# No identity matmuls in PE's waits, B's sum on GpSimd, output blocks and gelu in the first stage's own buffers

## The chip, the cores and the metric

One core of a Trainium2 chip runs the whole program. The metric is device time in microseconds (us), from one launch of the kernel. PE is TensorE, DVE VectorE, ACT ScalarE, POOL GpSimd, and SP the engine that only issues DMAs.

## What is computed

A hidden state of 256 tokens by 1024 columns goes through eight stages in fp32: an S5 state-space mixer with a gated output, a feed-forward block, a stick-breaking attention, a second feed-forward block, and then twice a hybrid layer with its feed-forward block. The change lies in the first stage, up to the gelu:

```python
dt = jnp.exp(log_dt)[:, None]
mag = jnp.exp(lam_re * dt)                       # 64 groups, 64 states each
lbar_re, lbar_im = mag * jnp.cos(lam_im * dt), mag * jnp.sin(lam_im * dt)
...
bb_re, bb_im = _cmul(coef_re[..., None], coef_im[..., None], b_re, b_im)
bu_re = jnp.einsum('blgh,gph->lbgp', u, bb_re)   # and bu_im
_, _, s_re, s_im = lax.associative_scan(_ssm_combine, (a_seq_re, a_seq_im, bu_re, bu_im), axis=0)
y = jnp.einsum('lbgp,ghp->blgh', s_re, c_re) - jnp.einsum('lbgp,ghp->blgh', s_im, c_im)
y = y.reshape(bsz, seq, D_MODEL) + d_skip * x
h = jax.nn.gelu(y)
val, gate = jnp.split(h @ w_glu, 2, axis=-1)
z = val * jax.nn.sigmoid(gate)
```

## The kernel before, in words

`s5_states` computes everything up to the gelu, and leaves the result transposed and split into a high and a low half (`xTh`, `xTl`). `main_stream` then runs all the large matmuls, three for each product (high by high, low by high, high by low). Its weights come in tiles of 512 KB: a DMA into one of the four buffers of the pool `raws`, a copy to the high half on ACT (`wh`), two subtractions for the low half on DVE (`wl`).

In `s5_states` the sequence is cut into 32 chunks of 8 tokens. The parts, with the names that the order uses:

- The start, in the order of the code: DMAs of the parameters, of B, C and x; powers 1 to 8 of lambda on DVE (`LR`), their sum and difference `PRs`, `PRd` in the PSUM tile `lt[0]`, and on ACT the negated real part `nPRr` in the PSUM tile `lt[1]` and copies `LRs`, `LRd` in SBUF. PE transposes B and C; ACT copies B to `Br`, `Bi`; PE sums both once more into `both`, which ACT copies to `Bs` (the real plus the imaginary part).
- `ug`, `ut`, `us`: x is regrouped (ACT), transposed (PE) and stored as `u` (ACT).
- For each of eight blocks of groups: three products `vp` on DVE (B times powers of lambda), their transposes `vt` on PE (four of 128x128 each), stores `vs` on ACT into `vT`; then `sm`, `sd`, `st`, `ss` (PE, ACT, PE, ACT) give the chunk states; `ss7` is the last.
- `cp`, `cs`: C times the coefficient, on DVE. `wp`: 24 products of C and powers of lambda on POOL, into the tiles `W` and `wd`; `dm` the skip blocks on POOL.
- `lp`, `lc`, `lw`: the response within a chunk (PE), copied into `kz` (ACT), and spread by 16 small DMAs for each half into the tile `lag`.
- `mg`, `bo`: the scan over the chunks, on DVE alone; its multipliers lie in `lt[1]` (`bp`, `bt` make them).
- For each half f: `tm` and three `om` on PE give the outputs, `os` copies them (the output blocks `yc`), `ot` transposes on PE, `og` is the gelu on ACT, `oh` and `ol` the two halves of the result. `sx` makes the difference of the states that the third `om` reads.
- `wd`, `wh`, `wl`: a first weight tile for `main_stream`, loaded and split within the stage.

The order of all these steps on each engine is written out in the table `ORDER`. An entry `=12` of it issues 12 matmuls of the identity with 64 columns of itself, into columns 448 to 511 of `lt[1]`, which nothing reads (line 728); there are 159 of them. A PSUM tile that PE writes is not read by DVE at the same time, whatever its columns. The four buffers of `raws` hold in turn `Bs` with the skip blocks, the first weight tile, the output blocks and the gelu of either half, and then the weights of `main_stream`.

The lines which the rows name: 249 transposes of B and C, 322 B's sum on PE, 341 and 357 lambda's powers on DVE, 409 `ug`, 415 `ut`, 461 `vp` and `wp`, 477 `Bd` (the difference of B's parts), 495 `vt`, 499 `vs`, 512 and 527 `sd` and `ss`, 563 to 566 `mg` and `bo`, 651 `tm`, 664 `om`, 685 `oh`, 717 `wl`, 728 the identity matmuls, 779 the weights' high half in `main_stream`, 822 to 824 its three matmuls.

Of the kernel before, what the change touches and what calls it, by code (L numbers as in the profile page):

```python
# [12 lines left out]
F32 = mybir.dt.float32  # L13
# [6 lines left out]
P = 128  # L20
# [146 lines left out]
cp00 cp01 =12 dt ug0 =29 ut0 cp10 vp01 ds cp11 vt01 bm ug1 us00 us01 vp02 wd vs01 ut1 us10 =1 vt02 vp00 dk vp12 vs02  # L167
vp10 cs2 vp11 vt00 ut2 vs00 bp0 vt12 vp22 dm vp20 us11 vs12 vt10 sm0 vt11 vp21 vs10 us20 wp12 vt22 sd0 vs11 vp30 ut3
vs22 st0 vp31 us30 ss0 vt21 vt20 vs21 vs20 cs1 bt0 cs0 lz1 wr0 wp02 sm1 vt31 vp40 lz0 wp22 vs31 wp32 vp32 wp31 vt30
vs30 wp01 sd1 vp42 wp20 lz2 wp21 vp41 sm2 sd2 vt40 vt32 vs40 wp11 st1 vs32 vp50 st2 wp30 wp00 vt42 ss1 lz3 wp10 vp52  # L170
vt41 vp60 bp1 ss2 sm3 vs42 vt52 vs41 vp61 wr1 wp62 vt50 sd3 vp51 vs52 sm4 wp40 bt1 vs50 vt60 wp71 st3 sd4 vs60 ss3 bp2
st4 ss4 us31 us21 wh0 vt61 vt51 wh1 vs51 vs61 vp70 lp0 lc110 vp62 lc010 wp70 lc000 vp72 vp71 wp61 lc101 lc100 vt62
vt71 lc011 wp60 vs62 lc111 wl1 =18 sm5 vt70 vs71 sd5 bp3 =4 vt72 lw1 wp41 wp42 wp72 lc001 vs70 wp51 vs72 =2 st5 ss5
sm6 mg00 sm7 sd6 wl0 st6 sd7 lw0 mg01 =4 st7 ss6 wp50 ss7 wp52 =5 lp1 mg02 lc310 mg10 lc300 mg11 lc301 lc311 lc200 lw3
lc201 mg12 lc211 bo0 bo1 bo2 bo3 lc210 =40 tm0 bo04 bo05 =12 om00 =1 om01 bo14 lw2 sx0 =1 om02 hd bo15 os01 os00 =12
ot01 ot00 sx1 og00 og01 oh01 =7 tm1 =1 om10 =1 om11 =1 om12 oh00 os10 os11 =8 ot11 og11 ot10 ol01 ol00 og10 oh10 oh11
ol10 ol11
# [3 lines left out]
def s5_states(nc, tc, a, V, S, G, T, const, raws, ats, hpool, mm_ps, tp_ps, xts, ident, load_h, **_):  # L181
# [11 lines left out]
    def buf(tag, shape):  # L193
        return z.tile(shape, F32, name=tag, tag=tag, bufs=BUFS[tag])
# [15 lines left out]
    with tc.manual_schedule(engines=PAP):  # L210
# [108 lines left out]
        both = tp_ps([P, SH, NGP])  # L319
        for hh in range(SH):  # L320
            for i, raw in enumerate(b_raw):
                T.matmul(both[:, hh, :], raw[:, :, hh], i32, start=(i == 0), stop=(i == 1))
        S.copy(Bs, both.rearrange("p h g -> p g h"))
# [43 lines left out]
        def step(name, fn, *args):  # L367
            steps[name] = lambda: fn(*args)

        def first(key, make):  # L370

            if key not in tl:
                tl[key] = make()
            return tl[key]
# [21 lines left out]
        def gelu(f):  # L396
            return first(("gel", f), lambda: raws.tile([P, 4, NC, TC], F32, name="raw", tag="raw"))
# [78 lines left out]

        step("bm", lambda: G.tensor_sub(Bd, Br, Bi))
# [19 lines left out]
        def v_store(i, k):  # L497
            vT = first(("vT", i), lambda: buf("vT", [P, 3, 4, P]))
            (V.tensor_copy if (i, k) in DVE_V else S.copy)(vT[:, k], tl["pv", i, k])
# [167 lines left out]
        def state_out_store(f, b):  # L667
            yc = first(("yc", f), lambda: raws.tile([P, TC, 8, SH], F32, name="raw", tag="raw"))
            (V.tensor_copy if f * b else S.copy)(yc.rearrange("p j (g e) h -> p g j e h", e=2)[:, :, :, b, :],
                                       tl["pc", f][b].rearrange("p g (j h) -> p g j h", h=SH))  # L670
# [53 lines left out]
        with tc.manual_schedule(engines={mybir.EngineType.DVE}):  # L724
            for name in ORDER.split():
                if name[0] == "=":
                    for _ in range(int(name[1:])):
                        T.matmul(lt[1][:, 448:], ident, ident[:, :64], start=True, stop=True)  # L728
                else:
                    steps.pop(name)()  # L730
# [816 lines left out]
```

## Time and profile before

| | us |
|---|---|
| median of 3 runs (1412.14 to 1417.54) | 1415.89 |
| the profiled execution | 1417.67 |
| its span in the trace | 1415.9 |
| PE busy in the span | 1382.7 (98%) |
| DVE, ACT, POOL busy | 905.5, 688.2, 80.3 |
| identity matmuls (line 728) busy on PE | 51.6 |

The first stage lasts until about 142 us of the span. A row of the timeline gives the start and the length of a group of like instructions, and behind it, in brackets, how long the engine stood idle before it and whose end it waited for. Matmuls overlap, so the length of one is not the step from one to the next: a row's length divided by its count is nearer to the step. Each fp32 matmul or transpose with an identity that is not a transposing one shows as two records, so the 12 matmuls of `=12` are 24 records. [...]

### The profile page before, as it was taken

Reading aid. Unit: us, or ns where it says so; the run is one execution under the profiler, and the core shown is the slowest. Engines: PE = TensorE matmul, PEld = TensorE weight load, DVE = VectorE, ACT = ScalarE, POOL = GpSimd, SP = SyncE. Lnnn points to the kernel's source line nnn. Section 1 sums busy time; section 2 is a strip of 40 time slices with the busy share of each in tenths; the row PEclk is TensorE's granted clock in tenths of the full one; section 3 lists DMA queues with packets and bytes.
Section 4 is the critical chain, followed back from the end, with each engine's and each line's share of the span. In section 5 each row is a group of like instructions: output and inputs, shape, how many; then the busy total and the mean of one; then the engine's idle time right before and its main releaser. Section 6 shows DMA issues by size and latency. Waiting matters only on the chain.

```text
span 1415.9 us, 21753 instructions
## 1 busy us (share of the span) xinstructions
PE 1382.7 (98%) x8009; PEld 1155.0 (82%) x8009; DVE 905.5 (64%) x1881; ACT 688.2 (49%) x1065; POOL 80.3 (6%) x149
## 2 busy tenths in 40 slices
PE   7988999999999999999999999999999999999998
PEld 7987878888888878888787888888888888888887
DVE  5472767555588686555699658655568866856463
ACT  1531654444468745444446545544545654545451
POOL 1420000000001110000020000000001000000000
PEclk9997999999999999999999999999999999999999
DMA  5163957555564436665455555646555554655551
GB/s 135 61 69 103 292 168 232 185 179 178 194 193 156 140 119 214 193 197 191 120 162 160 181 177 184 200 152 208 177 157 174 148 161 153 202 186 174 182 195 58
DMA packets 143403, 237.38 MB, mean 168 GB/s; under 512 B 15744, under 2 KB 84800, under 8 KB 142656
## 3 DMA queue, kind: packets, MB, share of 16 engines
q1 hardware_dynamic: 143296, 235.99, 53.8%
q8 instruction: 63, 1.03, 0.3%
q14 instruction: 44, 0.36, 0.1%
HBM read 228.35 MB, written 1.05 MB: 162 GB/s over the span
## 4 chain that ended last, share of the span: by engine, by line
PE 91%; DVE 5%; DMA 1%; ACT 1%; issue 1%; POOL 0%; SPq 0%; ACTq 0%; DVEq 0%; POOLq 0%
PE acc L824 8%; PE acc L823 8%; PE acc L822 8%; PE mm_ffn_g_t L823 5%; PE mm_ffn_g_t L824 5%; PE mm_ffn_g_t L822 5%; PE mm_ff_g_t L822 4%; PE mm_ff_g_t L824 4%; PE mm_ff_g_t L823 4%; PE lt L728 3%; PE tp L881 2%; PE mm_hy_t L823 2%; PE mm_hy_t L822 2%; PE mm_hy_t L824 2%; PE mm_s_g_t L822 1%; PE mm_hy_b_t L824 1%
## 5 line engine op out<-in xcount | busy, mean ns | idle before, releaser
L785 DVE TENSOR_TENSOR wl<-raw,wh 128x512 fp32r<-128x512 f32 (+1 forms) x834 | 541.8, 685 | 150.1 <-ACT wh L779 133.3
L779 ACT CAST wh<-raw 128x1024 fp32r<-128x1024 f32 (+1 forms) x417 | 436.4, 1048 | 246.7 <-DMA raw<-in_ffn_w_gu_dram 42.4
L822 PE MATMUL acc<-wh,bTh 128*128 128x512 f32 x544 | 213.2, 392 | 0.0
L823 PE MATMUL acc<-wh,bTl 128*128 128x512 f32 x544 | 211.9, 390 | 0.3
L824 PE MATMUL acc<-wl,bTh 128*128 128x512 f32 x544 | 212.1, 390 | 0.0
L822 PE MATMUL mm_ffn_g_t<-wh,xTh 128*128 128x512 f32 x352 | 140.5, 399 | 1.9 <-ACT xTh L867 1.9
L823 PE MATMUL mm_ffn_g_t<-wh,xTl 128*128 128x512 f32 x352 | 137.5, 391 | 0.4 <-DVE xTl L868 0.4
L824 PE MATMUL mm_ffn_g_t<-wl,xTh 128*128 128x512 f32 x352 | 137.4, 390 | 0.0
L868 DVE TENSOR_TENSOR bTl<-tp,bTh 128x256 fp32r<-128x256 f32 (+1 forms) x104 | 52.6, 512 | 124.4 <-ACT bTh L867 124.4
L823 PEld LDWEIGHTS acc<-wh,bTl 128*128 128x128 f32 x544 | 102.2, 188 | 21.7 <-DVE bTl L868 1.0
L824 PEld LDWEIGHTS acc<-wl,bTh 128*128 128x128 f32 x544 | 102.1, 188 | 21.3
L822 PEld LDWEIGHTS acc<-wh,bTh 128*128 128x128 f32 x544 | 102.2, 188 | 21.0 <-ACT bTh L867 0.3
L867 ACT CAST bTh<-tp 128x256 fp32r<-128x256 f32 (+1 forms) x104 | 45.3, 444 | 149.0 <-PE tp L881 135.6
L822 PE MATMUL mm_ff_g_t<-wh,xTh 128*128 128x512 f32 x256 | 102.6, 401 | 0.0
L824 PE MATMUL mm_ff_g_t<-wl,xTh 128*128 128x512 f32 x256 | 99.9, 390 | 0.0
L823 PE MATMUL mm_ff_g_t<-wh,xTl 128*128 128x512 f32 x256 | 99.7, 389 | 0.0
L822 PEld LDWEIGHTS mm_ffn_g_t<-wh,xTh 128*128 128x128 f32 x352 | 66.1, 188 | 14.9 <-ACT xTh L867 2.4
L823 PEld LDWEIGHTS mm_ffn_g_t<-wh,xTl 128*128 128x128 f32 x352 | 66.2, 188 | 13.8 <-DVE xTl L868 1.1
L824 PEld LDWEIGHTS mm_ffn_g_t<-wl,xTh 128*128 128x128 f32 x352 | 66.1, 188 | 13.8
L822 PE MATMUL mm_hy_t<-wh,xTh 128*128 128x512 f32 (+1 forms) x160 | 61.4, 384 | 0.8 <-DVE at L1328 0.6
L823 PE MATMUL mm_hy_t<-wh,xTl 128*128 128x512 f32 (+1 forms) x160 | 59.8, 374 | 1.5 <-DVE xTl L868 1.3
L824 PE MATMUL mm_hy_t<-wl,xTh 128*128 128x512 f32 (+1 forms) x160 | 59.8, 374 | 0.0
(475 smaller groups left out, 2136.0 us busy)
## 6 DMA issues: line engine op xcount, KB each, us to landing
raw<-in_w_ff_dram SPq DMA_DIRECT2D x128, 512.0 KB, 4.5
raw<-in_ffn_w_gu_dram SPq DMA_DIRECT2D x176, 256.0 KB, 4.1
raw<-in_w_in_dram SPq DMA_DIRECT2D x64, 512.0 KB, 4.4
raw<-in_ffn_w_down_dram SPq DMA_DIRECT2D x44, 512.0 KB, 4.9
raw<-in_ssm_w_glu_dram SPq DMA_DIRECT2D x32, 256.0 KB, 3.9
raw<-in_sb_w_qkv_dram SPq DMA_DIRECT2D x32, 256.0 KB, 3.8
raw<-in_w_out_dram SPq DMA_DIRECT2D x16, 512.0 KB, 4.3
raw<-in_ssm_w_out_dram SPq DMA_DIRECT2D x8, 512.0 KB, 4.5
```

Of the source, the lines that this page charges most:

```text
L728: T.matmul(lt[1][:, 448:], ident, ident[:, :64], start=True, stop=True)
L779: S.copy(wh, raw)
L785: V.tensor_sub(l2[:, sl], r2[:, sl], h2[:, sl])
L822: T.matmul(ps, xh[:, k], wh, start=first, stop=False)
L823: T.matmul(ps, xl[:, k], wh, start=False, stop=False)
L824: T.matmul(ps, xh[:, k], wl, start=False, stop=last)
L867: S.copy(hi, ps)
L868: V.tensor_sub(lo, ps, hi)
L881: T.transpose(pt[:, k, :], src[:, k * P:(k + 1) * P], ident)
```

## The change

All identity matmuls go, with the branch that issues them. B's sum goes from PE (32 matmuls in `both`, and a copy on ACT) to POOL, as one addition of `Br` and `Bi`. The output blocks `yc` take a buffer of `vT`, and the gelu one of `u`, so that both leave the pool `raws`. The table `ORDER` is written anew; two lines of it are shown.

```diff
 ORDER = """
-cp00 cp01 =12 dt ug0 =29 ut0 cp10 vp01 ds cp11 vt01 bm ug1 us00 us01 vp02 wd vs01 ut1 us10 =1 vt02 vp00 dk vp12 vs02
...
+ug1 vp12 ut2 vp11 cp10 cp00 bm vt12 bs ug0 us20 cp11 ut3 us21 cp01 vt11 vp10 vs12 cs2 vt10 wp12 us31 vp02 vp01 cs1
...
-        both = tp_ps([P, SH, NGP])
-        for hh in range(SH):
-            for i, raw in enumerate(b_raw):
-                T.matmul(both[:, hh, :], raw[:, :, hh], i32, start=(i == 0), stop=(i == 1))
-        S.copy(Bs, both.rearrange("p h g -> p g h"))
...
-            return first(("gel", f), lambda: raws.tile([P, 4, NC, TC], F32, name="raw", tag="raw"))
+            return first(("gel", f), lambda: buf("u", [P, 4, NC, TC]))
...
+        step("bs", lambda: G.tensor_add(Bs, Br[:, :NGP], Bi[:, :NGP]))
         step("bm", lambda: G.tensor_sub(Bd, Br, Bi))
...
-            vT = first(("vT", i), lambda: buf("vT", [P, 3, 4, P]))
+            vT = first(("vT", i), lambda: buf("vT", [P, 3 * 4 * P]).rearrange("p (k q n) -> p k q n", k=3, q=4))
...
-            yc = first(("yc", f), lambda: raws.tile([P, TC, 8, SH], F32, name="raw", tag="raw"))
+            yc = first(("yc", f), lambda: buf("vT", [P, 3 * 4 * P])[:, :TC * P].rearrange("p (j g h) -> p j g h", j=TC, g=8))
...
-                if name[0] == "=":
-                    for _ in range(int(name[1:])):
-                        T.matmul(lt[1][:, 448:], ident, ident[:, :64], start=True, stop=True)
-                else:
-                    steps.pop(name)()
+                steps.pop(name)()
```

PE's instructions from the transposes of C to the first transposes of a product `v`, before (lines 249 and 322 belong to the start, 434 is `dt`):

```order
L249 MATMUL pv<-ident,c_136 128x32 x16
L322 MATMUL tp<-ident,big_134 128x32 x32
L728 MATMUL lt_124<-ident 128x64 x12
L434 MATMUL tp<-ident,dpad 64x32 x2
L728 MATMUL lt_124<-ident 128x64 x29
L415 MATMUL tp<-ident,xTh 128x128 x4
L495 MATMUL pv<-ident,v 128x128 x4
```

The same place on PE now (the line numbers are those of the changed code: 248 was 249, 409 was 415, 490 was 495):

```order
L248 MATMUL pv<-ident,c_136 128x32 x16
L409 MATMUL tp<-ident,xTl 128x128 x4
L490 MATMUL pv<-ident,v 128x128 x4
L409 MATMUL tp<-ident,xTl 128x128 x4
L490 MATMUL pv<-ident,v 128x128 x8
```

The sum of B and the first 41 identity matmuls are gone from ahead of the first transposes, and the second half of x comes first.

PE's instructions from the end of `lp1` to the second half's `om`, before (624 ends `lp1`, 651 is `tm`, 664 `om`, 676 `ot`, 822 the first matmul of the gated unit):

```order
L624 MATMUL mm<-raw,pick 32x4x16 x8
L728 MATMUL lt_124<-ident 128x64 x40
L651 MATMUL mm<-lag_585,u 32x128 x32
L728 MATMUL lt_124<-ident 128x64 x12
L664 MATMUL mm<-big_587,c_1238 32x128 x32
...
L728 MATMUL lt_124<-ident 128x64 x12
L676 MATMUL tp<-ident,raw 128x128 x8
L728 MATMUL lt_124<-ident 128x64 x7
L822 MATMUL mm_s_g_t_1770<-wh,xTh 128x512
L651 MATMUL pv<-big_634,u 32x128 x32
```

The same place now (619 ends `lp1`, 646 is `tm`, 659 `om`, 671 `ot`, 813 the first matmul of the gated unit):

```order
L619 MATMUL mm<-raw,pick 32x4x16 x8
L646 MATMUL mm<-lag_438,u 32x128 x32
L659 MATMUL mm<-big_461,c_1102 32x128 x32
L659 MATMUL mm<-big_399,c_1102 32x128 x32
L659 MATMUL mm<-wd,gap 32x112 x32
L671 MATMUL tp<-ident,vT 128x128 x8
L813 MATMUL mm_s_g_t_1578<-wh,xTh 128x512
L646 MATMUL pv<-big_698,u 32x128 x32
```

The order of the real steps is the same, and nothing stands between them any more.

SP's queue around the spread DMAs of the chunk response (`lag`, `big` with `kz`), before (709 is the first weight tile, 150 the load of x for the residual, 887 a norm's gain, 776 the weights of `main_stream`, two DMAs for each tile):

```order
L709 DMA raw<-in_ssm_w_glu_dram 128x2x256 x2
L609 DMA lag_585<-kz 128x2048 x2
L609 DMA big_634<-kz 128x2048 x2
L633 DMA lag_585<-kz 16x2048
...
L150 DMA h<-in_x_dram 128x1024 x2
L887 DMA lng<-in_ln_mix_g_dram 128x1024
L776 DMA raw<-in_ssm_w_glu_dram 128x2x256 x8
```

The same queue now (704, 604, 628, 878 and 767 are the lines 709, 609, 633, 887 and 776 of before):

```order
L604 DMA lag_438<-kz 128x2048 x2
L704 DMA raw<-in_ssm_w_glu_dram 128x2x256 x2
L604 DMA big_698<-kz 128x2048 x2
L767 DMA raw<-in_ssm_w_glu_dram 128x2x256 x4
L628 DMA lag_438<-kz 16x2048 x2
...
L150 DMA h<-in_x_dram 128x1024 x2
L767 DMA raw<-in_ssm_w_glu_dram 128x2x256 x4
L878 DMA lng<-in_ln_mix_g_dram 128x1024
```

Four weight tiles of `main_stream` are now ahead of the norm's gain, which waits for the stage's end: two of them ahead of the spread, two behind the load of x.

## Rows read from the trace of the kernel before

**Rows 1.** Busy time by stretch of the span: start and end, then its length.

```profile
core 0: us, PE busy (x) PEld busy (x) DVE busy (x) ACT busy (x) POOL busy (x), PEclk, DMA share, GB/s
31.40:49.50 18.10, 18.05 (x86) 17.87 (x87) 1.89 (x3) 2.64 (x5) 0.00 (x0) 1.00 0.29 117
49.50:87.30 37.80, 35.00 (x658) 31.07 (x658) 28.98 (x55) 27.36 (x64) 24.48 (x25) 1.00 0.22 26
115.00:120.00 5.00, 5.00 (x24) 5.00 (x25) 1.39 (x2) 1.07 (x2) 0.00 (x0) 0.50 0.01 3
142.30:147.10 4.80, 4.80 (x11) 3.75 (x12) 4.80 (x8) 4.07 (x4) 0.00 (x0) 0.50 0.90 321
147.10:1416.00 1268.90, 1256.33 (x6206) 1038.79 (x6204) 830.86 (x1689) 637.68 (x964) 47.94 (x78) 1.00 0.55 175
```

**Rows 2.** Chain that ended last, 10 to 60 us: start, length, engine and line.

```profile
15.13 13.86 PE tp L322 x64
```

**Rows 3.** Timeline of VectorE, first stage: start, length, count, idle before.

```profile
12.38 1.17 DVE L341 TENSOR_SCALAR sm<-LR 128x32 f32<-128x32 f32 x1
...
17.38 0.43 DVE L357 TENSOR_TENSOR lt<-LR 128x256 f32<-128x256 f32 x1
...
32.00 0.69 DVE L461 TENSOR_TENSOR v<-Bi,lt 128x512 f32<-128x512 f32 x1 [12.40 <-ACT LRd L360]
...
74.44 5.09 DVE L717 TENSOR_TENSOR wl<-raw,wh 128x512 fp32r<-128x512 f32 x1 [0.87 <-PE pv L495]
...
88.05 0.70 DVE L563 TENSOR_TENSOR lt<-c,lt 128x512 f32<-128x512 f32 x1 [0.68 <-PE lt L728]
...
100.75 0.64 DVE L563 TENSOR_TENSOR lt<-c,lt 128x256 f32<-128x256 f32 x1 [3.05 <-PE lt L728]
...
104.87 0.69 DVE L566 TENSOR_TENSOR c<-lt,mt 128x512 f32<-128x512 f32 x1
```

**Rows 4.** Timeline of TensorE around the changes and the stage's end.

```profile
49.55 1.06 PE L415 MATMUL tp<-ident,xTh 128*128 128x128 f32 x4
...
53.51 0.60 PE L415 MATMUL tp<-ident,xTl 128*128 128x128 f32 x4
...
107.92 1.96 PE L664 MATMUL mm<-big,c 64*32 64x128 f32 x64
...
114.92 5.38 PE L728 MATMUL lt<-ident 128*128 128x64 f32 x24
...
124.35 0.50 PE L822 MATMUL mm_s_g_t<-wh,xTh 128*128 128x512 f32 x1 [0.20 <-ACT xTh L685]
...
127.17 1.16 PE L664 MATMUL pv<-big,c 64*32 64x128 f32 x64
...
131.52 2.00 PE L728 MATMUL lt<-ident 128*128 128x64 f32 x16
...
142.30 0.79 PE L822 MATMUL mm_s_g_t<-wh,xTh 128*128 128x512 f32 x1 [5.38 <-ACT wh L779]
```

**Rows 5.** Timeline of ScalarE, first stage.

```profile
31.59 0.37 ACT L360 COPY LRd<-lt 128x256 f32<-128x256 f32 x1
31.86 1.06 ACT L409 COPY xTh<-big 128x1024 f32<-128x1024 f32 x1
...
79.44 0.59 ACT L499 COPY vT<-pv 128x512 f32<-128x512 f32 x1 [2.47 <-PE mm L508]
...
82.89 0.39 ACT L512 ACTIVATE sls<-mm 128x256 f32<-128x256 f32 x1 [0.67 <-PE mm L508]
...
86.92 0.37 ACT L527 COPY c<-mm 128x256 f32<-128x256 f32 x1 [2.45 <-PE mm L517]
...
135.19 1.15 ACT L685 CAST xTh<-raw 128x512 fp32r<-128x512 f32 x2
...
141.20 3.88 ACT L779 CAST wh<-raw 128x1024 fp32r<-128x1024 f32 x4 [4.87 <-DMA raw<-in_ssm_w_glu_dram]
```

**Rows 6.** Identity matmuls, 31 to 50 and 91 to 101 us: ns min/median/max.

```profile
L728 PE MATMUL lt<-ident x82: 421/421/475, 31.4 to 49.3; 128*128 128x64 f32 x82
...
L728 PE MATMUL lt<-ident x80: 275/275/323, 91.6 to 100.4; 128*128 128x64 f32 x80
```

**Rows 7.** Timeline of GpSimd, first stage.

```profile
12.15 1.36 POOL L477 TENSOR_TENSOR Bd<-Br,Bi 128x528 f32<-128x528 f32 x1 [5.95 <-ACT Bi L317]
```

More of the change, by code (lines that the diff above doesn't have):

```diff
@@ L166 @@
 ORDER = """
-cp00 cp01 =12 dt ug0 =29 ut0 cp10 vp01 ds cp11 vt01 bm ug1 us00 us01 vp02 wd vs01 ut1 us10 =1 vt02 vp00 dk vp12 vs02
[L168 to L177, printed above, removed]
+ug1 vp12 ut2 vp11 cp10 cp00 bm vt12 bs ug0 us20 cp11 ut3 us21 cp01 vt11 vp10 vs12 cs2 vt10 wp12 us31 vp02 vp01 cs1
+vp20 vp00 us30 vs11 ut1 ut0 vt02 vs10 us11 vp21 us00 vt01 lz0 sm1 vs02 us10 vs01 wp31 sd1 dk vt20 vt00 vp22 vp41 st1
+dt vp40 vs20 lz1 wp21 vt21 vp31 wp32 vs00 us01 vt22 ss1 ds vs21 vs22 wp01 wr0 vp42 sm0 vt41 vt40 vp30 sm2 vs41 wp02
+vp32 vt42 cs0 wp22 vs40 dm vt31 sd0 st0 wd sd2 st2 vs42 wp11 vt30 vs31 ss0 vp51 vt32 sm4 vp61 vp62 wp20 ss2 vs30 vt61
+vs32 vt62 wr1 vs61 sm3 vt51 vs62 sd4 wp30 sd3 vp60 st4 vs51 wp00 st3 vt60 vp50 ss4 vp72 lz3 ss3 bp0 vp71 wp10 vt50 lz2
+wp42 bt0 vp70 wp51 wh0 bp1 bt1 vp52 lp0 wp52 vs60 vs50 lc000 lc110 lc111 lc100 vt52 mg00 wp72 vt71 lc010 lc011 vs52
+sm6 bp2 lc001 vs71 wp61 vt70 mg01 vt72 lc101 sd6 st6 wp71 vs70 vs72 wp60 wp41 wp50 sm5 ss6 wh1 wp62 sd5 sm7 sd7 wp70
+st5 wp40 st7 wl0 ss5 bp3 ss7 lp1 wl1 lc300 mg02 lc311 mg10 lc301 mg11 mg12 bo0 lc310 bo1 lc200 lc211 lw1 lw0 bo2 lc201
+bo3 lc210 bo04 bo05 lw3 tm0 om00 sx0 om01 om02 os01 bo14 os00 bo15 sx1 lw2 ot01 ot00 tm1 om10 hd og01 om11 om12 og00
+oh01 oh00 os10 os11 ot11 ol00 ol01 og11 ot10 og10 oh10 ol10 oh11 ol11
 """
```

## The prediction

> **What bounds the kernel now.** I first read the table of busy time by stretch [rows 1]. From 147.10 us to the end TensorE is busy 1256.33 of 1268.90 us, with its clock at the high level. The change leaves the order of instructions there as it was, so it can win nothing there, and lose only if the clock does. All of the gain must come from the 147 us ahead.
>
> There TensorE looks just as busy: 18.05 of 18.10 us between 31.40 and 49.50, and 35.00 of 37.80 in the stretch behind it [rows 1]. But the whole of the first of these is identity matmuls, whose result nobody reads, so a busy share says nothing here. What matters is whether anybody waits for TensorE while it does them. Three views answer that. The chain that ended last holds the 64 records of B's sum, 13.86 us from 15.13 on [rows 2]. VectorE's timeline shows that lambda's powers are done at 17.38 + 0.43 = 17.81, and that the first product `vp` starts only at 32.00, after 12.40 us of idleness; later `mg` waits 0.68 and 3.05 us for line 728 by name [rows 3]. On TensorE the first transposes of x start at 49.55, though their operand has been there since 31.86 + 1.06 = 32.92 [rows 4, 5]. So the queue of TensorE, full of work that nobody needs, sets this stage.
>
> The purpose that such matmuls can have is the clock. Identity matmuls take 421 ns in the median from 31 to 49 us, and 275 from 91 to 100 [rows 6]. The column of the granted clock says 1.00 for the first stretch, but I go by the durations: four transposes take 1.06 us at 49.55 and 0.60 at 53.51 [rows 4]. So 18 us of unbroken 64-column matmuls did not raise the clock, and it rose soon after the 128-column transposes began. At 115 to 120 us the column says 0.50 too. The fillers thus did not hold the clock through the stage, and that is why I charge little for their loss.
>
> **The change, part by part.** All is measured against the profiled execution, 1417.67 us, which stands 1.8 above the median.
>
> *Until the first transposes.* B's sum on GpSimd is one addition like `Bd`, which takes 1.36 us [rows 7]. While `Bd` ran, a step of lambda on 32 columns took VectorE 1.17 us [rows 3], so the second addition may hold the chain of powers as long: 0 to 1.36, and I take 1.3, because it stands right behind `Bd`, in the middle of that chain. Then come a short copy on ACT, 0.37, and the regrouping of x, 1.06 [rows 5]: 17.81 + 1.3 + 0.4 + 1.06 = 20.6 instead of 49.55. That is **-29.0**.
>
> [...]
>
> *First transposes to the last chunk state `ss7`.* This took 86.92 + 0.37 - 49.55 = 37.74 us. ACT waits 2.47, 0.67 and 2.45 us in it for matmuls that stand behind fillers [rows 5], 5.6 in all. Against that I put 0.6 for the order that is new: a VectorE instruction behind a GpSimd product can take 5.09 us (`wl` at 74.44) instead of 0.69 [rows 3], a loss of 0 to 4.4, but VectorE is busy only 28.98 of 37.80 us and has room for most of it [rows 1]. **-5.0**, with `ss7` at about 53.4. Bounds: nothing gained, or down to ACT's 27.36 busy us [rows 1], a gain of 10.4.
>
> *`ss7` to the first `om`.* From 87.29 to 107.92 there are 20.6 us [rows 4, 5]. VectorE's scan begins at 88.05 behind a wait for the fillers, waits 3.05 us at 100.75, and ends at 104.87 + 0.69 = 105.56 [rows 3]. Without the fillers in that bank the chain is (100.75 - 3.05 - 88.05) + (105.56 - 100.75) = 14.5 us, and `om` follows it at once: **-6.1**.
>
> *First `om` to the first gated matmul.* 124.35 - 107.92 = 16.43 us. Twelve fillers (24 records) take 5.38, and two pairs 0.69 each [rows 4]. Behind the twelve lie the copies of the output blocks, some 1.3 us that now show: 5.38 + 1.38 - 1.3 = **-5.4**. The first `om` is slow already (1.96 against 1.16 for the second half's [rows 4]) and stays so.
>
> *To the end of the second half's `om`.* Fillers left there are three singles or pairs; at the 0.114 to 0.22 us of a step that the rows of line 728 give, I take **-1.0**.
>
> *From there to the main matmuls.* They resume at 142.30, after an idle 5.38 us [rows 4]. Eight fillers cost 2.00 [rows 4] and hide about 1.0 of the copies: -1.0. The first cast of the weights starts at 141.20 after a wait of 4.87 us on its DMA, while ACT was through with `oh` at 135.19 + 1.15 = 136.34 [rows 5]. These DMAs stand, before, behind the norm's gain and the buffers of the gelu; now four tiles are issued ahead of it. The cast can then start some 0.8 us after `oh`, when the stage's tiles are free: 141.20 - 137.1 = -4.1. **-5.1**. `wl` in its new place may wait 0.5: **+0.5**.
>
> *The clock behind it.* 11 matmuls take 4.80 us after the resumption, at the low level, 0.436 each; later 1256.33 / 6206 = 0.202 [rows 1]. If the shorter idle time leaves the clock up, they give back 11 x 0.234 = 2.6; some idleness remains, so I take **-2.2**, with bounds 0 and 2.6.
>
> Sum: -29.0 - 5.0 - 6.1 - 5.4 - 1.0 - 5.1 + 0.5 - 2.2 = -53.3, and 1417.67 - 53.3 = **1364** us.
>
> **The rivals.**
>
> *The clock falls in the tail of the stage.* TensorE now idles some 8 us before `tm0`. For it: the first `om` is slow before too, at 1.96. Against: the clock came back in the second half (1.16) with hardly more than transposes behind it [rows 4]. If it stays low until the main matmuls, three `om` cost 3 x 0.80, `tm1` about 1.1 as its like, the transposes `ot` 2 x 0.46, and the 2.2 are not given back: +6.6, so **1371**. [...]
>
> *The weights come late anyway.* If the early tiles don't help, as the cast waits for something else, 4.1 and 2.2 are lost: **1371**. VectorE behind GpSimd's products has the same size: with 4.4 lost once, 1368 to 1369.
>
> *The clock stays low through the whole stage.* 28 groups of four transposes would take 0.46 more each, 12.9, if all lie on the path, and the tail 6.6: **1384**. Against it: it was the transposes at 49.55 behind which the clock rose [rows 4], and these come closer together now.
>
> *Slower than before.* The clock stays low on into the main stream. Each matmul there then costs 0.234 us more, and the 53.3 us are gone after 53.3 / 0.234 = 228 of them, about 99 us at the low clock. With 400, 1364 + 94 = **1458**. Against it: before, the rise came 4.80 us after the resumption [rows 1], and nothing in that stream changes.
>
> *No change.* The fillers and the sum would have to lie beside something that takes as long; VectorE's 12.40 us of idleness [rows 3] speak against it.
>
> **How the numbers follow.** The forecast gets 0.66, with a range of its own from 1358 to 1369; a low clock in the tail 0.14; late weights or VectorE behind GpSimd 0.09; the low clock through the stage 0.08; slower 0.02; no change 0.01. The lower end of the whole range is the forecast with the sum's 1.3 and the other 1.1 of locks hidden, and five more of the ten us of the second term: 1356. The upper is the low clock and late weights together, without the 2.2 twice: 1364 + 6.6 + 4.1 + 4.4 = 1379, which leaves out the low clock through the stage and the slower case, and a little of either tail. Half a per cent, some 7 us, is about what a measurement of this kernel can tell from no change; every case but the last two lies further below it: faster 0.97, same 0.01, slower 0.02.
>
> **What the profile of the changed kernel would show.** The first transposes at about 20.6, `ss7` done near 53, the first `om` near 68, the first gated matmul near 79, and the main matmuls resumed at 90 to 91 without a wait on a weight's DMA; VectorE held for about 1.3 us at 13.5 to 14.8, behind B's sum; the four transposes of a group at 0.60 and not 1.06; the main stream as long as before. I would be wrong by most if the stretch from the first transposes to `ss7` grew: VectorE behind GpSimd, or transposes at the low clock, are what to look for there.

## The result and the profile after

The changed kernel takes 1372.57 us (median of 4 runs, 1372.04 to 1379.16) against 1415.47 of the kernel before beside it: the ratio is 0.971, with a 95% interval of 0.9675 to 0.9745. That lies in the predicted range of 1356 to 1379, 8.6 us above the predicted 1364 and above the likeliest case's own range. The profiled execution takes 1372.04 us, 45.6 less than that of before; its span is 1370.3.

TensorE's timeline of the changed kernel, around the marks that [rows 4] showed of before (line numbers of the changed code: 409 first transposes, 503 `sm`, 646 `tm`, 659 `om`, 671 `ot`, 813 to 815 the main matmuls):

```profile
20.55 1.12 PE L409 MATMUL tp<-ident,xTl 128*128 128x128 f32 x4 [5.42 <-ACT xTl L403]
49.14 1.08 PE L503 MATMUL mm<-vT,u 128*32 128x128 f32 x32 [1.94 <-ACT kz L623]
66.39 4.26 PE L646 MATMUL mm<-lag,u 128*32 128x128 f32 x64 [4.22 <-ACT kz L623]
71.12 2.03 PE L659 MATMUL mm<-big,c 64*32 64x128 f32 x128 [0.47 <-DVE c L561]
75.30 0.58 PE L659 MATMUL mm<-wd,gap 64*32 64x112 f32 x23 [1.61 <-issue]
77.06 1.36 PE L671 MATMUL tp<-ident,vT 128*128 128x128 f32 x8 [1.18 <-ACT vT L664]
80.28 0.79 PE L813 MATMUL mm_s_g_t<-wh,xTh 128*128 128x512 f32 x1 [1.85 <-ACT xTh L680]
81.00 3.66 PE L646 MATMUL pv<-big,u 128*32 128x128 f32 x64
87.79 2.84 PE L659 MATMUL pv<-big,c 64*32 64x128 f32 x98 [2.54 <-issue]
91.52 0.76 PE L659 MATMUL pv<-wd,gap 64*32 64x112 f32 x35 [0.27 <-issue]
98.07 0.50 PE L813 MATMUL mm_s_g_t<-wh,xTh 128*128 128x512 f32 x1 [1.33 <-ACT wh L770]
...
118.50 0.39 PE L813 MATMUL acc<-wh,bTh 128*128 128x512 f32 x1
```

No row of an identity filler is left, and the first transposes stand at 20.55 instead of 49.55. The first `om` is at 71.12 instead of 107.92, the first gated matmul at 80.28 instead of 124.35, and the main matmuls resume at 98.07 instead of 142.30. But three of these rows have a wait that says "issue", 1.61, 2.54 and 0.27 us in the middle of a run of like matmuls: TensorE waited for nothing that the profile can name. Two more such waits, 0.98 and 2.19 us, stand ahead of them in `lp`, at 44.96 and 61.67. `tm` of the second half takes 3.66 us.

VectorE, ScalarE and GpSimd in the changed kernel, the rows that answer to [rows 3], [rows 5] and [rows 7]:

```profile
13.47 1.30 POOL L471 TENSOR_TENSOR raw<-Br,Bi 128x512 f32<-128x512 f32 x1
...
13.56 1.29 DVE L327 TENSOR_TENSOR mt<-LR 128x64 f32<-128x64 f32 x1
14.88 0.21 DVE L327 TENSOR_TENSOR mt<-LR 128x64 f32<-128x64 f32 x1
18.44 0.43 DVE L351 TENSOR_TENSOR lt<-LR 128x256 f32<-128x256 f32 x1
19.59 0.69 DVE L455 TENSOR_TENSOR v<-Br,lt 128x512 f32<-128x512 f32 x1 [0.71 <-ACT LRd L354]
...
56.29 0.37 ACT L522 COPY c<-mm 128x256 f32<-128x256 f32 x1 [0.26 <-PE mm L512]
```

B's sum holds one of lambda's products, which takes 1.29 us beside it, where the next one of the same shape takes 0.21; lambda's powers are done at 18.44 + 0.43 = 18.87; the first product of B starts at 19.59 instead of 32.00; and `ss7` ends at 56.29 + 0.37 = 56.66.

Busy time by stretch in the changed kernel, columns as in [rows 1], and under it the main stream of the kernel before, each from its first matmul of `acc` on:

```profile
20.55:56.70 36.15, 32.36 (x598) 26.77 (x598) 28.26 (x61) 28.64 (x66) 23.96 (x25) 0.95 0.41 110
77.75:84.58 6.83, 4.97 (x69) 3.66 (x67) 0.00 (x0) 2.33 (x4) 0.00 (x0) 0.50 0.88 295
80.28:92.35 12.07, 9.19 (x257) 7.42 (x257) 0.03 (x1) 0.11 (x1) 0.00 (x0) 0.68 0.34 117
118.50:1370.30 1251.80, 1239.38 (x6129) 1024.54 (x6127) 818.76 (x1669) 627.46 (x951) 48.05 (x78) 1.00 0.55 175
...
164.20:1415.90 1251.70, 1239.23 (x6129) 1024.69 (x6127) 818.85 (x1667) 627.12 (x951) 47.94 (x78) 1.00 0.55 174
```

The main stream is as long as before, 1251.8 against 1251.7 us: the whole difference was made ahead of the first matmul of `acc`, at 118.50 instead of 164.21, and that is 45.7 us. From 77.75 to 84.58 the granted clock is 0.50 of full speed; in the second half's `tm` and `om`, 80.28 to 92.35, its mean is 0.68.

Set side by side, the stretches of the prediction, in us of the profiled executions:

| stretch | before | predicted | after | predicted change | measured change |
|---|---|---|---|---|---|
| to the first transposes | 49.55 | 20.6 | 20.55 | -29.0 | -29.0 |
| to the end of `ss7` | 37.74 | 32.7 | 36.11 | -5.0 | -1.6 |
| to the first `om` | 20.63 | 14.5 | 14.46 | -6.1 | -6.2 |
| to the first gated matmul | 16.43 | 11.0 | 9.16 | -5.4 | -7.3 |
| to the end of the second half's `om` | 7.24 | 6.2 | 12.00 | -1.0 | +4.8 |
| to the resumption | 10.71 | 6.1 | 5.79 | -4.6 | -4.9 |
| from there to `acc` | 21.91 | 19.7 | 20.43 | -2.2 | -1.5 |
| sum | | | | -53.3 | -45.7 |

Two rows miss: 3.4 us in the stretch to `ss7`, and 5.8 in the second half's `tm` and `om`.

### The profile page after: what moved, and what is told of

Same layout as the page of the kernel before. It is cut to its first block, busy times and chain, and to the rows that moved or that the text cites. A ratio compares the mean times of both kernels' runs of the same rounds, so it can differ in the third digit from the quotient of the medians.

```text
span 1370.3 us, 20985 instructions
## 1 busy us (share of the span) xinstructions
PE 1324.8 (97%) x7627; PEld 1095.0 (80%) x7627; DVE 902.2 (66%) x1881; ACT 688.1 (50%) x1064; POOL 81.2 (6%) x150
## 4 chain that ended last, share of the span: by engine, by line
PE 89%; DVE 6%; ACT 1%; issue 1%; DMA 1%; POOL 1%; SPq 0%; ACTq 0%; DVEq 0%; POOLq 0%
PE acc L814 9%; PE acc L815 9%; PE acc L813 9%; PE mm_ffn_g_t L814 6%; PE mm_ffn_g_t L815 6%; PE mm_ffn_g_t L813 6%; PE mm_ff_g_t L813 4%; PE mm_ff_g_t L815 4%; PE mm_ff_g_t L814 4%; PE tp L872 2%; PE mm_hy_t L814 2%; PE mm_hy_t L813 2%; PE mm_hy_t L815 2%; PE mm_hy_b_t L815 1%; PE mm_hy_b_t L813 1%
```

## The experiments

Each ran beside the kernel before. The table has the median, the ratio to it with its interval, and two figures from the profile: where the first matmul of `acc` stands (how long the stage and the first 96 main matmuls took), and how long the program still took from there.

| kernel | median us | ratio, interval | `acc` at | from there |
|---|---|---|---|---|
| changed | 1372.57 | 0.971, 0.9675 to 0.9745 | 118.50 | 1251.8 |
| e1, fillers alone removed | 1386.43 | 0.9783, 0.9744 to 0.9822 | 129.53 | 1256.5 |
| e2, sum on TensorE | 1385.88 | 0.9781, 0.975 to 0.9812 | 128.56 | 1256.7 |
| e3, blocks in `raws` | 1376.54 | 0.9716, 0.9685 to 0.9747 | 120.87 | 1253.8 |
| e4, 8 narrow matmuls | 1367.71 | 0.9652, 0.9621 to 0.9684 | 114.83 | 1251.0 |
| e5, 24 fillers in waits | 1369.71 | 0.9664, 0.9622 to 0.9706 | 112.58 | 1251.5 |
| e6, and 12 narrow ones | 1368.74 | 0.9646, 0.9622 to 0.9669 | 113.76 | 1253.6 |
| e7, and 11 in the tail | 1367.06 | 0.9646, 0.9614 to 0.9677 | 113.79 | 1250.4 |
| e8, `kz` on VectorE | 1373.14 | 0.9676, 0.9649 to 0.9703 | 118.34 | 1253.7 |
| e9, x held back | 1368.07 | 0.9656, 0.963 to 0.9682 | 115.03 | 1250.1 |
| e10, e7 with x held back | 1368.64 | 0.9658, 0.9633 to 0.9683 | 115.60 | 1252.3 |
| e11, e10 with B late | 1366.87 | 0.9642, 0.9613 to 0.9672 | 113.95 | 1252.7 |
| e12, e9 with B late | 1370.30 | 0.9673, 0.9657 to 0.9689 | 114.37 | 1256.9 |

The last column should be one number, since nothing was changed there, and it varies by 7 us. Part of it can be read in the granted clock. The stretch 470 to 480 us of e9, and under it the same of e12:

```profile
470.00:480.00 10.00, 9.78 (x45) 7.96 (x44) 8.78 (x17) 3.79 (x5) 0.99 (x1) 1.00 0.56 164
...
470.00:480.00 10.00, 7.40 (x28) 5.60 (x26) 8.72 (x17) 5.19 (x6) 0.99 (x1) 0.83 0.54 188
```

In e12 the clock is low for a third of the 10 us, in e9 it is not; from 670 to 680 us the means are 0.83 and 1.00 again. So a difference of a few us between two medians may come from the main stream, and below the place of `acc` tells what an edit did to the stage. It comes from one trace of each kernel, and such places vary too: the changed kernel, e3, e5 and e9 run the same instructions up to the transposes ahead of `sm6`, which start at 46.10, 45.40, 45.26 and 45.85 us. A difference of less than 1 us in `acc` says nothing here.

**The parts of the change, one at a time.** First e1: all `=n` go from the order of the kernel before, and nothing else.

```diff
-cp00 cp01 =12 dt ug0 =29 ut0 cp10 vp01 ds cp11 vt01 ...
+cp00 cp01 dt ug0 ut0 cp10 vp01 ds cp11 vt01 ...
```

> The kernel before with its 159 identity matmuls taken out of the order, and nothing else: B's sum stays on TensorE, the output blocks and the gelu stay in raws. Theory (the fillers held VectorE and ScalarE up by standing in TensorE's queue): the first transposes then wait for B's sum alone, at about 32.9 us instead of 49.55, and the stretches behind gain as in the changed kernel, while the wait for the first weights stays: about 29 us less, 1386 to 1390. Rival (the fillers kept the clock up, and the gain came from B's sum and the buffers): less than 10 us, 1406 or more.

It took 1386.43 us, 32 less than the kernel before (1418.65) in its run, and its first transposes wait for ScalarE's regrouping behind B's sum, at 32.95:

```profile
32.95 1.12 PE L403 MATMUL tp<-ident,xTh 128*128 128x128 f32 x4 [3.62 <-ACT xTh L397]
```

So the theory holds: the removal of the fillers alone is worth 34.7 us in the stage (164.21 to 129.53). Then e2, the changed kernel with B's sum back on TensorE:

```diff
+        both = tp_ps([P, SH, NGP])
+        for hh in range(SH):
+            for i, raw in enumerate(b_raw):
+                T.matmul(both[:, hh, :], raw[:, :, hh], i32, start=(i == 0), stop=(i == 1))
+        S.copy(Bs, both.rearrange("p h g -> p g h"))
-        step("bs", lambda: G.tensor_add(Bs, Br[:, :NGP], Bi[:, :NGP]))
```

> The changed kernel with B's sum back on TensorE (32 matmuls and a copy on ScalarE) in place of the addition on GpSimd. Theory (the sum was the gate of the regrouping of x behind the fillers): the first transposes move from 20.55 to about 32.9, all behind them follows, +12 us, about 1384. Rival (what follows is bound by GpSimd's products or by TensorE, which catch up): under +5, at most 1377.

```profile
14.96 14.03 PE L321 MATMUL tp<-ident,big 32*128 32x32 f32 x64
32.96 1.12 PE L414 MATMUL tp<-ident,xTl 128*128 128x128 f32 x4 [3.97 <-ACT xTl L408]
```

1385.88 us: the sum takes 14.03 us on TensorE, the first transposes stand at 32.96, 12.4 later than in the changed kernel, and `acc` comes 10.1 later. The theory holds; some 2 us of the delay are made good behind it. Then e3:

```diff
-            return first(("gel", f), lambda: buf("u", [P, 4, NC, TC]))
+            return first(("gel", f), lambda: raws.tile([P, 4, NC, TC], F32, name="raw", tag="raw"))
...
-            yc = first(("yc", f), lambda: buf("vT", [P, 3 * 4 * P])[:, :TC * P].rearrange("p (j g h) -> p j g h", j=TC, g=8))
+            yc = first(("yc", f), lambda: raws.tile([P, TC, 8, SH], F32, name="raw", tag="raw"))
```

> The changed kernel with the output blocks and the gelu back in the buffers of raws. Theory (the early weights are what the second half's buffers had held back): TensorE waits again for the cast behind the weights' DMA, some 4 to 5 us at the end of the stage, about 1377. Rival (the weights are not the last to arrive, or the early loads cost as much elsewhere, by delaying other transfers): within 1.5 us of the changed kernel.

```profile
99.35 0.80 PE L813 MATMUL mm_s_g_t<-wh,xTh 128*128 128x512 f32 x1 [6.43 <-ACT wh L770]
```

1376.54 us, as the theory has it: TensorE waits 6.43 us for the first cast, where the changed kernel waits 1.33. But `acc` comes only 2.4 later, not 5. The rest was won elsewhere: with the weights not yet loading, the pause of 2.54 us in the second half's `om` was gone.

No run has the new order of the steps alone. But e1 and e2 both lack the fillers and have B's sum on TensorE, and differ in the buffers and the order; `acc` stands at 129.53 and 128.56, so that the two together are worth about 1 us.

**The pauses without a name.** e4 puts eight matmuls of one column ahead of the first transposes:

```diff
+        spare = tp_ps([P, 64])
+        for _ in range(8):
+            T.matmul(spare[:, :1], ident, ident[:, :1], start=True, stop=True)
         squares, powers_at, copies = [], [], []
```

> The changed kernel with 8 one-column matmuls (16 records) on TensorE ahead of the first transposes, where it idles for 5.4 us; their result is read by nobody. Theory (the pauses of 1.6 and 2.5 us inside the om groups, for which the profile names no releaser, are waits for the next 16 KB of TensorE's own instructions, which come every 128 pairs of weight load and matmul): each pause moves 16 records earlier in the program, that in om10 from its 29th to its 13th record, that in om02 from its 42nd to its 26th. Rival (they wait for data or for another engine): they stay at the same records. The time within 2 us of the changed kernel by either.

Busy time by stretch once more, from the start to the end of each pause; what counts is the number behind PEld, the weight loads up to there. The changed kernel, then e4, then the kernel before up to its one pause (0.21 us), and the pause of e4 in `om02` on TensorE's timeline:

```profile
0.00:44.90 44.90, 30.92 (x468) 27.40 (x468) 36.10 (x112) 24.85 (x56) 27.07 (x51) 1.00 0.67 178
0.00:61.60 61.60, 43.16 (x850) 36.85 (x851) 49.24 (x147) 34.71 (x76) 32.11 (x56) 0.97 0.63 145
0.00:75.20 75.20, 50.48 (x1104) 42.79 (x1104) 62.36 (x178) 39.32 (x84) 32.11 (x56) 0.93 0.65 136
0.00:87.70 87.70, 57.40 (x1229) 47.87 (x1230) 64.36 (x180) 42.72 (x90) 32.11 (x56) 0.90 0.66 143
0.00:91.50 91.50, 60.85 (x1357) 50.99 (x1358) 64.36 (x180) 42.72 (x90) 32.11 (x56) 0.89 0.63 137
...
0.00:59.00 59.00, 44.53 (x850) 38.82 (x851) 48.35 (x146) 34.48 (x76) 32.14 (x56) 1.00 0.64 151
0.00:73.30 73.30, 51.40 (x1104) 44.54 (x1104) 62.17 (x178) 39.08 (x84) 32.14 (x56) 0.95 0.68 139
0.00:86.40 86.40, 61.05 (x1357) 52.21 (x1358) 63.89 (x180) 42.49 (x90) 32.14 (x56) 0.90 0.68 145
...
0.00:131.15 131.15, 115.81 (x1742) 107.64 (x1742) 66.68 (x180) 42.53 (x91) 31.36 (x55) 0.93 0.39 80
...
73.33 0.96 PE L662 MATMUL mm<-wd,gap 64*32 64x112 f32 x39 [2.02 <-issue]
```

In the changed kernel the pauses stand behind 468, 851, 1104, 1230 and 1358 weight loads. In e4 they stand behind 851, 1104 and 1358 too, although 16 more records lie ahead: each came 16 records earlier in the program, in `om02` 39 of its 64 records are left behind the pause instead of 23. The distances are 383, 253, 126 and 128: three, two, one and one times 127 or so. In the kernel before, the pause is behind 1742, another 384 on from 1358. What could come at such a count is TensorE's own instructions: on the page of before, the larger of the two queues called "instruction" has 63 packets and 1.03 MB, 16 KB each, and TensorE 8009 matmuls, 127 for each packet, so I take it for TensorE's. The packets in the trace beside the pauses, in us:

```
kernel   last load ahead, next   packet of 16 KB    next load behind the packet's end
changed  43.63   44.96           42.51 to 43.51     1.45
changed  59.16   61.68           59.30 to 60.22     1.46
changed  73.34   75.29           72.99 to 73.95     1.34
changed  84.88   87.79           85.22 to 86.34     1.45
changed  90.74   91.52           88.83 to 90.00     1.52
e4       56.73   59.04           56.76 to 57.71     1.33
e4       70.96   73.33           70.98 to 71.86     1.47
e4       85.67   86.45           83.79 to 85.07     1.38
```

Each pause ends 1.3 to 1.5 us after such a packet has landed. The theory holds: by these counts and packets the pauses are waits for the next block of instructions, 16 KB for some 127 weight loads and as many matmuls.

The time fell as well, to 1367.71, 4.9 us below the changed kernel where I had allowed 2, and `acc` by 3.7: the pauses at 468 and 1230 are gone, 1.33 and 2.92 us between two loads. The packet for 1230 moved at 75.10 in e4, before the weights were issued (76.46), and at 85.22 in the changed kernel, behind them. Why one block comes late showed in e9, which holds the loads of x for the residual back behind the second half's outputs:

```diff
             h.append(hpool.tile([P, DM], F32, name="h", tag="h"))
+            V.memset(h[t][:, :1], 0.0)
...
-... tm1 om10 hd og01 om11 om12 og00
+... tm1 om10 og01 om11 om12 og00
-oh01 oh00 os10 os11 ot11 ...
+oh01 oh00 os10 os11 hd ot11 ...
```

> The changed kernel with the two loads of x for the residual (1 MB of the 2 MB that move from 76.8 to 86 us) held back until the second half's outputs are copied, and nothing else. Theory (these loads stand ahead of TensorE's next 16 KB of instructions, which landed at 86.3 us, 5 us after they could be asked for): the block lands before it is needed, the pause of 2.5 us in om10 goes to 0.5 or less, the fall of the clock at 88.0 with it, and the time is 1368 to 1370, unless x, now ahead of the fifth weight tile, gives 1 to 3 us of it back behind the stage. Rival (the pause has nothing to do with the loads): it stays at 2 to 3 us at the same record.

DMA queues (packets, MB, share of 16 engines) of the changed kernel from 76 to 85.2 us and from 85.2 to 87, and of e9 from 76 to 85; then TensorE in e9:

```profile
q1 hardware_dynamic: 1568, 2.25, 83.8%
...
q8 instruction: 1, 0.02, 3.9%
...
q1 hardware_dynamic: 1254, 1.16, 46.5%
q8 instruction: 1, 0.02, 0.9%
...
80.51 3.66 PE L636 MATMUL pv<-big,u 128*32 128x128 f32 x64
84.10 2.97 PE L649 MATMUL pv<-big,c 64*32 64x128 f32 x128
```

In the changed kernel 2.25 MB of x and weights go first, and the block moves at 85.22; in e9 it moves at 81.16, among 1.16 MB of data, and the first 128 records of `om1` run through in 2.97 us. In both, the block moves as the loads run out: the busy share of the DMA engines falls from 0.63 (84 to 84.5 us) to 0.25 (85 to 85.2) in the changed kernel, and from 0.90 (81 to 81.2) to 0.33 (81.2 to 81.6) in e9. 1368.07 us, `acc` 3.5 earlier: the theory holds for this pause. For the others nothing of the kind was tried.

**The clock, and waits that the fillers covered.** e5 puts fillers back at two places where TensorE waits anyway, into a buffer that nobody reads then; e6 adds narrow ones ahead of the first transposes; e7 adds two groups around `ot`.

```diff
 # e5
-vs52 sm6 bp2 ... lw3 tm0 om00
+vs52 =8 sm6 bp2 ... lw3 =16 tm0 om00
...
+                if name[0] == "=":
+                    spare = tp_ps([P, 64])
+                    for _ in range(int(name[1:])):
+                        T.matmul(spare, ident, ident[:, :64], start=True, stop=True)
 # e6: as e5, and 12 of the narrow matmuls of e4
 # e7: as e6, and
-ot01 ot00 tm1
+=4 ot01 ot00 =7 tm1
```

> The changed kernel with 24 identity matmuls back at two places where TensorE waits anyway, 8 ahead of sm6 (1.9 us behind the copies of kz) and 16 ahead of tm0 (4.2 us), written to a PSUM buffer that VectorE does not read then. Theory (what the change lost is the clock and TensorE's own instructions): the low clock of 50.4 to 53.9 goes (-1.5), tm0 is fast but not on the path, and the 48 records ahead shift the instruction blocks so that the next one is asked for ahead of the large loads and the pause of 2.5 us in om10 goes; the pause of 1.6 in om02 stays. 1366 to 1369. Rival (any filler delays what stands behind it, as before): 1372 or more.

> The fillers of the run with 24 of them, and 12 one-column matmuls ahead of the first transposes, 72 records ahead of om00 in all. Theory of the instruction blocks: the block that is missing in om02 is asked for during tm0, while TensorE waits for VectorE's bo, and its pause of 1.6 to 2.4 us goes too; the pause in the last om, 0.3 to 0.8, may stay. 1364 to 1367. Rival (the pauses stand for something else): as with 24.

> The fillers of the run with 36, and 11 more around the transposes ot of the first half, where TensorE waits 1.2 and 1.9 us for ScalarE. Theory of the clock: if it stays at the high level there, tm1 takes 2.0 instead of 3.6 us: 1.5 to 2 us below the run with 36. Rival: the fall of the clock has its cause in the idle times ahead or comes all the same, and tm1 stays at 3.6: within 0.7 of it.

TensorE at `sm6` in e5, and at the second half's `tm` and `om` in e7, with the granted clock behind e7's pause:

```profile
46.19 1.90 PE L713 MATMUL tp<-ident 128*128 128x64 f32 x16
48.29 1.08 PE L492 MATMUL mm<-vT,u 128*32 128x128 f32 x32 [0.20 <-ACT kz L612]
...
77.08 2.01 PE L638 MATMUL pv<-big,u 128*32 128x128 f32 x64 [0.57 <-DMA big<-kz]
82.70 2.07 PE L651 MATMUL pv<-big,c 64*32 64x128 f32 x65 [2.54 <-issue]
86.70 0.25 PE L651 MATMUL pv<-wd,gap 64*32 64x112 f32 x1 [0.61 <-issue]
...
82.50:85.90 3.40, 3.20 (x128) 3.16 (x128) 0.00 (x0) 0.00 (x0) 0.00 (x0) 0.50 0.18 58
```

In e5 the wait ahead of `sm6` is 0.20 us instead of 1.94, because the fillers stand in it: from the start of the transposes ahead of it `sm6` comes 3.03 us later (45.26 to 48.29), and 3.04 in the changed kernel. So these fillers cost nothing and shorten nothing. The clock does not fall behind the wait, and `ss7` ends at 55.08 instead of 56.66. Of these 1.6 us, `sm6` itself is 0.85 earlier, which comes from ahead of the fillers; from the start of `sm6` to the end of `ss7` it is 6.79 us for 7.52, so the low clock there had cost 0.7. That the fillers kept the clock up is not shown: e3, e4 and e9 have no fillers there, wait 1.94 to 2.00 us, have no fall, and take 6.78 to 6.79.

`acc` comes at 112.58, the best of all, and the rival's 1372 or more did not come. But the pauses did not go as expected: the one in `om02` went, and another, 2.81 us between two loads, came in the second half's `om`, at the boundary of 1358 weight loads. In e6 it stayed, 2.62, where I had allowed 0.3 to 0.8. In e7 the second half's `tm` takes 2.01 us, for 3.02 in e6 and 3.66 in the changed kernel, as the theory of the clock has it; e5, without the fillers around `ot`, has 2.03 as well, so e7 alone does not show that they did it. The pause behind it is 2.54, the clock falls behind that, and `acc` is where e6 had it. The median is 1.7 below e6's, as the theory said, but that lies in the main stream (1250.4 for 1253.6). What the faster matmuls won, the next block of instructions took: the rival's time for another reason than the rival's. e10 asks whether the loads cause that as well; it is e7 with the edit of e9.

> The run with 35 identity matmuls in TensorE's waits and 12 narrow ones ahead, with the two loads of x held back as well. Theory: its pause of 2.9 us in the second half's om, at record 64, shrinks to under 1, with the clock at the high level throughout; 1363 to 1365. Rival (with the clock high the blocks are used up faster than they can come, loads or not): the pause stays over 2, 1366 to 1368.

It has the same pause between the same loads, 2.90 us from one to the next, and 1368.64 us. The rival holds so far that x is not the cause: TensorE uses up a block sooner than the next comes, x or not. The weights are not excluded: 1.08 MB of them and of the last of `kz` move from 77 to 83 us, and the block moves at 82.96.

e8 takes the other way to the wait ahead of `sm6`:

```diff
-            S.copy(kz[32 * n:32 * n + 32, c].rearrange(
+            (V.tensor_copy if n < 2 and e else S.copy)(kz[32 * n:32 * n + 32, c].rearrange(
```

> The changed kernel with four of the eight copies of kz behind lp0 on VectorE instead of ScalarE. Theory (sm6 waits 1.9 us for these copies, and the clock falls behind that wait): the wait shrinks to about 0.5, the fall at 50.4 goes, ss7 is done 2 to 3 us earlier: 1369 to 1371. Rival (VectorE's scan, which stands behind the copies, pays for it, or the wait is not on the path): within 1 us of the changed kernel.

```profile
48.00 1.08 PE L503 MATMUL mm<-vT,u 128*32 128x128 f32 x32 [1.45 <-ACT kz L623]
...
45.60 0.69 DVE L623 COPY kz<-mm 32x512 f32<-32x512 f32 x1 [1.67 <-PE mm L619]
```

The wait is 1.45 us, and `ss7` ends at 55.53, 1.1 earlier; but VectorE waits 1.67 us for the first of its copies, and the first `om`, which waits for VectorE's scan, is only 0.3 us earlier. `acc` at 118.34: the rival holds.

**GpSimd beside lambda's powers.** e11 is e10 with B's sum on VectorE and `Bd` later; e12 is e9 with the same edit, without any filler.

```diff
-        step("bs", lambda: G.tensor_add(Bs, Br[:, :NGP], Bi[:, :NGP]))
+        step("bs", lambda: V.tensor_add(Bs, Br[:, :NGP], Bi[:, :NGP]))
...
-ug1 vp12 ut2 vp11 cp10 cp00 bm vt12 bs ug0 us20 cp11 ut3 us21 cp01 vt11 vp10 vs12 cs2 vt10 wp12 us31
+ug1 vp12 ut2 vp11 cp10 cp00 vt12 ug0 us20 cp11 ut3 us21 cp01 vt11 bs vp10 vs12 cs2 vt10 wp12 bm us31
```

> As the run before it in this call, and B's sum on VectorE (one addition of 0.6 to 0.7 us) behind the first products, its difference Bd on GpSimd behind the first wp. Theory (the two additions on GpSimd held lambda's powers up by 1.0 us each, at 12.4 and 13.6): the first transposes start at about 18.6 instead of 20.56, 1.5 to 2 us less than the run before it. Rival (VectorE's products are the next to be late, or x's regrouping is): less than 0.7 us.

> The changed kernel with the two loads of x held back and no fillers at all, and B's sum on VectorE behind the first products, Bd on GpSimd behind the first wp. Theory (the two additions on GpSimd held lambda's powers up by 1.0 us each; in the run before, the first products were 2.06 us earlier, but 24 narrow records on TensorE, which end at 20.2, hid it): the first transposes start at 18.5, ss7 and all behind it 1.5 to 2 us earlier than in the run with x held back alone: 1366 to 1367. Rival (what follows, GpSimd's wp or the blocks of instructions, gives it back): 1367.5 or more.

All engines in e11, and TensorE in e12:

```profile
15.05 5.28 PE L349 MATMUL tp<-ident 128*128 128x1 f32 x24
17.53 0.69 DVE L448 TENSOR_TENSOR v<-Br,lt 128x512 f32<-128x512 f32 x1 [0.71 <-ACT LRd L344]
20.19 1.09 PE L402 MATMUL tp<-ident,xTl 128*128 128x128 f32 x4
...
18.49 1.11 PE L399 MATMUL tp<-ident,xTl 128*128 128x128 f32 x4 [3.36 <-ACT xTl L393]
47.35 1.74 PE L493 MATMUL mm<-vT,u 128*32 128x128 f32 x32 [1.94 <-ACT kz L613]
```

In e11 the first product of B is at 17.53 instead of 19.59, but the 24 narrow records, 5.28 us from 15.05, were still on TensorE: my own filler hid the gain, and the first transposes are only 0.4 us earlier. Median and `acc` are 1.8 and 1.6 below e10's all the same, the theory's size, but e10 has a pause of 1.94 us behind 216 weight loads where e7, with the same instructions up to there, has 0.56: e11 tells neither way. In e12 the transposes start at 18.49, 2.06 us earlier, so the two additions on GpSimd do hold lambda's powers by 2 us together. Of the 2.06, `ss7` keeps 1.0 and `acc` 0.7 against e9: the wait ahead of `sm6` is 1.94 again, and this time with the clock down behind it (7.29 us from `sm6` to the end of `ss7`, for 6.78 in e9). Against the changed kernel, where the clock falls there too, `ss7` is the whole 2.0 earlier. So the stage gave some back, as the rival has it, but in part through a fall of the clock that the edit need not have caused; the time, 1370.30, decides nothing, since e12's main stream is 6.8 us longer than e9's.

All but e1 to e3 and e8 have `acc` 2.9 to 5.9 us earlier than the changed kernel, and lower medians, by 2.3 to 5.7 us. e4, with eight narrow matmuls in a wait, is the smallest edit, 1367.71 us. For six of these eight the interval of the ratio still overlaps that of the changed kernel, and between them the intervals don't decide.

## Why the prediction was right, and which steps were not

Its direction and size came from the right reading: the fillers kept others waiting. e1 shows it alone, 34.7 us in the stage; e2 shows that B's sum was the next to be late, 10.1; e3 that the buffers are worth 5.1 of wait at the end (6.43 against 1.33), and 2.4 in the place of `acc`. The steps *until the first transposes* (20.55 for 20.6, with B's sum costing 18.87 - 17.81 = 1.1 for the 1.3 charged), *`ss7` to the first `om`* (-6.2 for -6.1) and *from there to the main matmuls* (-4.9 for -4.6) came out as worked. The whole range holds the result; the likeliest case's own, 1358 to 1369, misses it by 3.6 us, and two steps that failed were in part made up by one that did better than worked.

*First transposes to `ss7`* failed at the sentence that ACT waits 5.6 us "for matmuls that stand behind fillers". One group of fillers covered a real wait: about where 18 of them stood before, `sm6` needs the buffers that ScalarE's copies of `kz` free, and the changed kernel still waits 1.94 us there. The clock falls behind that wait, which costs 0.7 us from `sm6` to `ss7`; e9 has the same instructions and the same 1.94 us there and no such fall, and its `ss7` ends at 55.66, 1.0 us earlier, so the fall is not certain. The pause at 468 weight loads adds some 1.3 us between two loads, of which the profile puts 0.98 down as waiting. These are about the missing 3.4 (1.94 + 0.7 + 0.98 = 3.6). How much each weighs was not separated: e3 and e9, without the fall, take 34.6 and 35.1 us for this stretch instead of 36.1, with pauses of 1.45 and 1.63 at 468.

*To the end of the second half's `om`* failed by 5.8 us: the step counted the fillers left there, -1.0, and nothing for what TensorE would then wait for or how fast it would run. The first cause, which the prediction did not name, is the pauses for instructions, 2.54 and 0.27. e9 takes the longer one away and gets 3.3 us back in this stretch (79.79 to 88.51 us is 8.72 for 12.00). The other 2.5 is about what the clock explains: in e9 `tm` takes 3.66 us, where e7 has 2.01 at the high level, and the 128 records of `om` behind it 2.97, for 2.03 in the first half of the changed kernel. The rival *the clock falls in the tail* put 1371 on this, near the result, but for half of it the mechanism is another, so that its number is luck in part. It had been given 0.14 on the ground that the clock came back before "with hardly more than transposes behind it", and that misread the trace of before. Between 114.92 and 124.35 us stand the 24 filler records of [rows 4], the transposes, and 14 records more; and the granted clock had been low there for 17 us, with TensorE all but fully busy:

```profile
121.80 2.35 PE L728 MATMUL lt<-ident 128*128 128x64 f32 x14
...
106.20:123.20 17.00, 16.76 (x245) 15.23 (x244) 5.81 (x10) 2.20 (x5) 0.00 (x0) 0.50 0.19 65
```

*First `om` to the first gated matmul* was better than worked, -7.3 for -5.4, against a pause of 1.61: `tm0` now runs at the low clock, 4.26 us, beside VectorE's scan where it costs nothing, and the first half's `om`, slow before at 1.96 us for 64 records, now take 2.03 for 128. "Stays so" was wrong there. (The two pairs of 0.69 us that the step takes from [rows 4] are not among its rows; the trace has them at 109.81 and 112.31.)

That B's sum would hold lambda's powers is borne out: 1.29 us for a product beside the sum, 0.21 for the next one without it. That the clock falls when TensorE idles, which the rival in the tail and the step *the clock behind it* took for granted, the runs show in part only. In the changed kernel TensorE waits 1.18 and 1.85 us around `ot`, and the clock is at 0.50 from 77.75 to 84.58. But before, with fillers in these waits, it was at 0.50 from 106.20 to 123.20; and fewer matmuls did not mean a low clock in the main stream, where it was up from the resumption on (1.00 from 99.13 to 118.50, and 0.23 us from one matmul to the next, for 0.44 behind the resumption before [rows 1]).

## What to carry to other kernels

Work that nobody needs is free only while nobody waits behind it: read who stands behind it, in its queue and at its buffers, and not the busy share (here it cost 34.7 us of the stage, e1). When it goes, look for the real waits that it had covered. Put back in one of these alone it cost nothing here (3.03 us to `sm6` for 3.04), but that it keeps the clock up is not shown. Where runs of short matmuls then go faster, count what TensorE must fetch for them, and keep bulk loads away from that moment (the wait of 2.54 us in `om` was gone when 1.16 MB moved there instead of 2.25, e9).

## What the runs showed of the hardware

TensorE waited for its own instructions, as far as counts and packets tell. One packet of 16 KB came for each 127 weight loads with their matmuls (63 for 8009 before) and took about 1 us (0.9 to 1.3 in the table of packets), and work went on 1.3 to 1.5 us after its end. The main matmuls, at 0.23 us each, use one up in some 29 us, an estimate (127 x 0.23); in the changed kernel no wait of theirs says "issue". `om`, 128 records in 2.03 us, uses one up in 2 us by the same estimate, and in the changed kernel waited 1.61, 2.54 and 0.27 us at the three boundaries that fall in it. With 2.25 MB of loads in the way the packet came 4.2 us behind the start of the second half's `tm`, with 1.16 MB, in e9, 0.65 us behind it. How early such a block is asked for was not measured.

The main stream of the same instructions took 1250.1 to 1256.9 us. In some executions the clock falls in it for a few us, near 480, 680 or 1043 us (to 0.50 from 675.08 to 678.50 in the changed kernel). It does not in e4, e5, e7 and e9 (1250.1 to 1251.5 us); it falls this once in the changed kernel, and once in e10 and e11 (1251.8 to 1252.7), twice in e3, e6 and e8 (1253.6 to 1253.8) and three times in e1 and e2 (1256.5 and 1256.7). Only e12, with two falls and 1256.9, does not fit. Why the clock falls there in one execution and not in another stays open.
